# Sums of squares from the columns, the memory split ahead of the weights, and the weights' low part last

## The chip, the cores and the metric

The kernel runs on one core of a Trainium2 chip. The metric is the device time of one execution in microseconds. The engines are TensorE (PE; its weight loads are PEld), VectorE (DVE), ScalarE (ACT), GpSimd (POOL) and SyncE (SP), which here only issues loads.

## What is computed

One layer of a hybrid decoder for 256 tokens of width 2048, with 256 memory tokens, in float32. What matters here is the start:

```python
def rms_norm(x, w):
    xf = x.astype(jnp.float32)
    y = xf * lax.rsqrt(jnp.mean(xf * xf, axis=-1, keepdims=True) + NORM_EPS)
    return (y * w.astype(jnp.float32)).astype(x.dtype)
...
        h = rms_norm(x, norm_w[layer])
        proj = h @ w_in[layer]
...
        mem_n = rms_norm(mem, mem_norm_w[layer])
        o_mem = memory_cross_attention(mem_q..., mem_n, w_mem_kv[layer])
```

`memory_cross_attention` multiplies `mem_n` by `w_mem_kv` (2048 x 2048; the left half gives the keys, the right half the values). After that come a stick-breaking attention, a state-space branch, three gates, an output projection with a residual, and a last norm. The change touches none of those.

## The kernel before

**Products.** Every float32 matrix is split into a high part that TensorE takes as it is and a low part, the rest. A product is three: high by high, high by low, low by high. `split` (L142) does it: ScalarE copies the high part (L146), VectorE subtracts it from the source (L150, or L152 with a scale). For weights these tiles are `raw`, `wh` and `wl` (four buffers of `raw`, three of each of the others).

**Order.** The order of the work on each engine is that of the program (`manual_schedule`). The program is cut into chunks: one load of 512 KB of weights, its split, its products, and then a call of `pump` (L185), which runs the side work that has come due. `defer(fn, n)` (L172) puts a function n pumps ahead. A list `lanes` holds generators of which one step runs at every second pump.

**The start.** The memory and x lie transposed in 16 tiles of 128 features by 256 tokens, here called columns 0 to 15. ScalarE's queue loads `head` (the gains `memw` and memory column 0, `mem0`) and then memory columns 1, 2 to 3 and 4 to 5 (`mload`, L491 to L493). TensorE runs ten products of ones meanwhile (`keep_warm`, L108). `gemm_values` (L437) then makes the values in 16 steps k, each with 128 rows of the weights for all 1024 value columns: SyncE loads the weights (L446, for k=0 in two halves `g`), `split` splits them, and between or after that `along(k)` (L416) splits the memory's columns of step k and starts other loads. The products run over both halves g and both token blocks t, three for each (L456 to L458), twelve a step. The accumulators are two of TensorE's accumulator tiles.

**The norms.** The memory's and x's row scales are not applied to the factors but later. For them `row_squares` loads mem and x a second time, by rows (`load_rows`, L368, on ScalarE's queue), ScalarE squares and sums them (`squares`, L380), and `scale_steps` (L384) makes the mean, raises it to the power -1/2 on GpSimd (128x2, L389), multiplies it into a diagonal (`dg`, L393), and spreads it over the partitions with a product by ones (`rbc`, L396), copied to `rbc_m` or `rbc_x` (L398). `rs_mem`, one scale per row, is used when the values leave their accumulators (`to_split_rows`, L288, three and four pumps after the last step). `rbc_x` scales the columns of x (`scale_pair`, L474), which are then split into `hT` (`split_pair`).

**After that** two sets of eight chunks make the keys (`gemm`, L249, lines L269 to L271) and the next ones take `hT`. A chunk there holds two steps of k for 512 columns and has 12 products as well.

Of the kernel before, what the change touches and what calls it, by code (L numbers as in the profile page):

```python
# [41 lines left out]
def trunk_kernel(  # L42
# [55 lines left out]
    ones = const.tile([P, P], F32, name="ones")  # L98
    nc.gpsimd.memset(ones, 1.0)
    ident = const.tile([P, P], F32, name="ident")  # L100
# [22 lines left out]
                            pattern=[[1, P]], channel_multiplier=-1)  # L123

    rs_mem = const.tile([P, 2], F32, name="rs_mem")
    rs_x = const.tile([P, 2], F32, name="rs_x")
# [15 lines left out]
    def split(*parts):  # L142


        for hi, _, src, scale in parts:
            nc.scalar.activation(hi, src, AF.Copy, **({} if scale is None else {"scale": scale}))  # L146
        for hi, lo, src, scale in parts:
            h32 = hi.bitcast(F32)
            if scale is None:
                nc.vector.tensor_tensor(lo, src, h32, ALU.subtract)  # L150
            else:
                nc.vector.scalar_tensor_tensor(lo, src, scale, h32, ALU.mult, ALU.subtract)  # L152
# [212 lines left out]
    def split_cols(raw, dst, w, k0):  # L365
        split(*[(*dst.at(k), raw[k // 8][:, k % 8], w[:, k:k + 1]) for k in (k0, k0 + 1)])

    def load_rows(src, q):  # L368

        cs = slice(q * GW, (q + 1) * GW)  # L370
        if q % 2:
            r = [ta([P, GW], "rows") for _ in range(2)]
            for t in range(2):
                nc.scalar.dma_start(r[t], src[t * P:(t + 1) * P, cs])
            return r
        r = t4([P, 2, GW], "rows")
        nc.scalar.dma_start(r, src[:, cs].rearrange("(t p) n -> p t n", p=P))
        return [r[:, t] for t in range(2)]

    def squares(r, ss, q):  # L380
        for t in range(2):
            nc.scalar.activation(r[t], r[t], AF.Square, accum_out=ss[:, t, q:q + 1])

    def scale_steps(rs, rbc, ss):  # L384

        ms = small([P, 2], "ms")
        nc.vector.tensor_reduce(ms, ss, AX.X, ALU.add)
        nc.vector.tensor_scalar(ms, ms, 1.0 / D, EPS, ALU.mult, ALU.add)
        nc.gpsimd.tensor_tensor(rs, ms, mhalf, ALU.pow)  # L389
        yield  # L390
        dg = tq([P, 2, P], "dg")
        for t in range(2):
            nc.vector.tensor_scalar(dg[:, t], ident, rs[:, t:t + 1], None, ALU.mult)  # L393
        yield
        pb = bank([P, T], "rbc")
        nc.tensor.matmul(pb, ones, dg.rearrange("p t k -> p (t k)"), start=True, stop=True)  # L396
        yield
        nc.vector.tensor_copy(rbc, pb)  # L398
        yield


    memT = Cols(NKT, "memT")
    hT = Cols(NKT, "hT")
    mraw, mload = load_cols(mem_cols[:, NKT:], "mraw")
    xraw, xload = load_cols(x_cols, "xraw")
    ss_m = const.tile([P, 2, 4], F32, name="ss_m")
    ss_x = const.tile([P, 2, 4], F32, name="ss_x")

    vh = slot([P, 2, 1024], F32R, "vh")
    vl = slot([P, 2, 1024], F32R, "vl")  # L410

    def row_squares(src, ss, q):
        r = load_rows(src, q)
        defer(lambda: squares(r, ss, q), 3)

    def along(k):  # L416

        if k == 0:
            split((*memT.at(0), mem0, memw[:, 0:1]))
        else:  # L420
            split((*memT.at(k), mraw[k // 8][:, k % 8], memw[:, k:k + 1]))
            if k % 2 and 1 < k < 12:
                mload(k + 3, k + 5)
            if k % 2 and 3 <= k < 10:
                row_squares(mem, ss_m, k // 2 - 1)
            if k in (10, 12, 13, 14):
                row_squares(x, ss_x, (10, 12, 13, 14).index(k))
        if k == 6:
            nc.sync.dma_start(wcols, w_cols)
        if k == 12:  # L430
            defer(lambda: lanes[0].append(scale_steps(rs_mem, rbc_m, ss_m)), 1)
        if k == NKT - 2:
            defer(lambda: scale_x(scale_steps(rs_x, rbc_x, ss_x)), 3)
            for q in range(0, NKT, 4):
                defer(lambda q=q: xload(q, q + 4), 1 + q // 2)

    def gemm_values():  # L437

        acc = [psA.tile([P, 2, GW], F32, tag="acc", name=nm("acc"), bufs=2) for _ in range(2)]
        for k in range(NKT):  # L440
            raw, wh, wl = (stage.tile([P, 2, GW], dt, tag=n, name=nm(n), bufs=b) for n, dt, b in
                           (("raw", F32, RAWB), ("wh", F32R, 3), ("wl", F32R, 3)))
            src = w_mem_kv[k * P:(k + 1) * P, 1024:2048].rearrange("p (g n) -> p g n", n=GW)
            parts = [slice(0, 1), slice(1, 2)] if k == 0 else [slice(0, 2)]
            for g in parts:
                nc.sync.dma_start(raw[:, g], src[:, g])  # L446
            for n, g in enumerate(parts):
                split((wh[:, g], wl[:, g], raw[:, g], None))
                if n == 0:
                    along(k)  # L450
            lh, ll = memT.at(k)
            first, last = k == 0, k == NKT - 1
            for g in range(2):
                for t in range(2):
                    a, tt = acc[g][:, t], slice(t * P, (t + 1) * P)
                    nc.tensor.matmul(a, lh[:, tt], wh[:, g], start=first, stop=False)  # L456
                    nc.tensor.matmul(a, lh[:, tt], wl[:, g], start=False, stop=False)  # L457
                    nc.tensor.matmul(a, ll[:, tt], wh[:, g], start=False, stop=last)  # L458
            pump()
        for g in range(2):  # L460
            defer(lambda g=g: to_split_rows(vh, vl, g * GW, rs_mem)(
                [acc[g][:, t] for t in range(2)]), LATE + g)

    x_ready = []

    def scale_x(steps):

        for _ in steps:
            defer(lambda: scale_x(steps), 1)
            return  # L470
# [18 lines left out]
    head = tb([P, NKT + T], "head")  # L489
    memw, mem0 = head[:, 0:NKT], head[:, NKT:]  # L490
    nc.scalar.dma_start(head, mem_cols[:, 0:NKT + T])  # L491
    for k0, k1 in ((1, 2), (2, 4), (4, 6)):
        mload(k0, k1, nc.scalar)  # L493
    nc.scalar.preload_act_table_set("silu_and_others")

    gemm_values()
# [302 lines left out]
    pair = []  # L799
# [259 lines left out]
    g = 3  # L1059
# [60 lines left out]
```

## Time and profile before

| | us |
|---|---|
| median of 3 runs (1211.16 to 1211.69) | 1211.44 |
| the profiled execution | 1211.59 |
| its span | 1209.9 |
| TensorE busy in it | 1199.0 |
| first useful product (k=0) | 6.08 |
| first product of k=1 | 10.36 |
| first product of k=2 | 14.03 |

The span runs from the first to the last instruction. A row of the timeline gives the start, the duration, the engine, the line in the kernel, the operation, out<-in by the program's names, the size, and in brackets how long the engine stood idle before and what released it. A row of waits reads "who waited <- for what: total, times, longest". Rows of groups end in busy time, mean ns of one operation and idle time before. A DMA queue's row gives packets, MB and the share of the 16 DMA engines; q1 is SyncE's queue, q10 ScalarE's. A row by windows gives for a stretch its length, the busy time of PE, PEld, DVE, ACT and POOL, the granted TensorE clock, the DMA share and GB/s. All times are microseconds from the start of the span.

### The profile page before, as it was taken

The numbers are of one execution on the slowest core, as the hardware profiler recorded it, in microseconds if no ns is written. First come the engines' busy times: TensorE is split into PE (matmuls) and PEld (weight loads), VectorE is DVE, ScalarE is ACT, GpSimd is POOL, SyncE is SP. The second block draws the span as 40 slices with busy tenths as digits, with TensorE's granted clock in tenths as the row PEclk, the third lists the DMA queues.
The fourth block names the chain that finished last, engine by engine and source line by source line (L and its number), as shares of the span: only waits on it lengthen the run. The fifth ranks groups of instructions, "written<-read, shape, count | busy, mean of one in ns | idle before, by whom it ended". The sixth has DMA issues, their size and how long they took to land.

```text
span 1209.9 us, 15621 instructions
## 1 busy us (share of the span) xinstructions
PE 1199.0 (99%) x5820; PEld 1005.8 (83%) x5820; DVE 791.6 (65%) x1035; ACT 634.1 (52%) x844; POOL 52.5 (4%) x50
## 2 busy tenths in 40 slices
PE   9999999999999999999999999999999999999997
PEld 7888888888888888888888888888888888888886
DVE  5686664546564555888887858677777655556752
ACT  6754443354355444545655756484757534444541
POOL 0100000000000000010100000000000010110101
PEclk9999999999999999999999999999999999999999
DMA  9977787887666777665668676667756677778751
GB/s 320 363 229 228 215 244 235 251 232 214 197 192 194 218 224 226 185 189 169 180 179 261 210 226 214 212 204 220 229 177 202 204 221 222 228 219 293 252 203 70
DMA packets 169820, 264.66 MB, mean 219 GB/s; under 512 B 11984, under 2 KB 67472, under 8 KB 169616
## 3 DMA queue, kind: packets, MB, share of 16 engines
q1 hardware_dynamic: 134304, 227.41, 61.6%
q10 hardware_dynamic: 35440, 36.26, 9.2%
q8 instruction: 45, 0.74, 0.2%
q14 instruction: 31, 0.25, 0.1%
HBM read 249.45 MB, written 14.19 MB: 218 GB/s over the span
## 4 chain that ended last, share of the span: by engine, by line
PE 97%; issue 1%; DMA 1%; ACT 0%; DVE 0%; SPq 0%; POOLq 0%; POOL 0%; ACTq 0%
PE acc L269 25%; PE acc L271 25%; PE acc L270 25%; PE acc L229 10%; PE acc L233 5%; PE acc L457 1%; PE acc L458 1%; PE acc L456 1%; PE y L874 1%; DMA raw<-in_w_mem_kv_dram 1%; PE dtp L518 0%; PE acc L1074 0%; PE acc L1072 0%; PE acc L1073 0%; PE spo L708 0%
## 5 line engine op out<-in xcount | busy, mean ns | idle before, releaser
L150 DVE TENSOR_TENSOR wl<-raw,wh 128x1024 fp32r<-128x1024 f32 (+1 forms) x409 | 504.4, 1236 | 309.4 <-ACT wh L146 307.9
L146 ACT ACTIVATE wh<-raw 128x1024 fp32r<-128x1024 f32 (+1 forms) x409 | 431.4, 1056 | 426.8 <-PE acc L271 337.1
L269 PE MATMUL acc<-wh,hT 128*128 128x512 f32 x896 | 350.9, 392 | 0.0
L270 PE MATMUL acc<-wl,hT 128*128 128x512 f32 x896 | 348.9, 389 | 0.3 <-DVE wl L150 0.3
L271 PE MATMUL acc<-wh,hT 128*128 128x512 f32 x896 | 348.9, 389 | 0.0
L271 PEld LDWEIGHTS acc<-wh,hT 128*128 128x128 f32 x896 | 168.2, 188 | 35.4
L270 PEld LDWEIGHTS acc<-wl,hT 128*128 128x128 f32 x896 | 168.3, 188 | 34.4 <-DVE wl L150 0.7
L269 PEld LDWEIGHTS acc<-wh,hT 128*128 128x128 f32 x896 | 168.3, 188 | 33.9 <-issue 0.3
L229 PE MATMUL acc<-hT,wh 128*128 128x512 f32 x512 | 161.6, 397 | 0.0
L233 PEld LDWEIGHTS acc<-hT,wl 128*128 128x128 f32 x512 | 96.2, 188 | 22.7
L233 PE MATMUL acc<-hT,wl 128*128 128x256 f32 x512 | 100.7, 278 | 0.0
L229 PEld LDWEIGHTS acc<-hT,wh 128*128 128x128 f32 x512 | 78.1, 189 | 0.1
L269 PE MATMUL acc<-wh,oD 128*128 128x512 f32 x128 | 49.8, 389 | 0.0
L270 PE MATMUL acc<-wl,oD 128*128 128x512 f32 x128 | 49.8, 389 | 0.0
L271 PE MATMUL acc<-wh,oD 128*128 128x512 f32 x128 | 49.8, 389 | 0.0
L748 DVE SCALAR_TENSOR_TENSOR cT<-cu,wcols,cT 128x255 f32<-128x255 f32 (+2 forms) x96 | 46.4, 483 | 3.4
L963 POOL TENSOR_TENSOR merged<-merged,sig 128x512 f32<-128x512 f32 x16 | 25.8, 1637 | 512.3 <-DVE sig L962 512.3
L269 PE MATMUL acc<-wh,mT 128*128 128x512 f32 x96 | 37.4, 390 | 0.0
L271 PE MATMUL acc<-wh,mT 128*128 128x512 f32 x96 | 37.4, 389 | 0.0
L270 PE MATMUL acc<-wl,mT 128*128 128x512 f32 x96 | 37.4, 389 | 0.0
L689 POOL TENSOR_TENSOR lm<-lm,sp 128x384 f32<-128x384 f32 x8 | 11.5, 1433 | 391.6 <-DVE sp L688 389.5
L269 PEld LDWEIGHTS acc<-wh,oD 128*128 128x128 f32 x128 | 24.0, 188 | 5.0
(243 smaller groups left out, 1298.8 us busy)
## 6 DMA issues: line engine op xcount, KB each, us to landing
raw<-in_w_in_dram SPq DMA_DIRECT2D x288, 512.0 KB, 4.4
raw<-in_w_branch_ssd_dram SPq DMA_DIRECT2D x32, 512.0 KB, 4.9
raw<-in_w_mem_kv_dram SPq DMA_DIRECT2D x31, 512.0 KB, 6.0
raw<-in_w_out_dram SPq DMA_DIRECT2D x24, 512.0 KB, 5.6
scratch<-blocks ACTq DMA_DIRECT2D x23, 512.0 KB, 4.2
raw<-in_w_branch_mem_dram SPq DMA_DIRECT2D x16, 512.0 KB, 4.9
raw<-in_w_branch_sb_dram SPq DMA_DIRECT2D x16, 512.0 KB, 5.0
turned<-scratch ACTq DMA_DIRECT2D x60, 128.0 KB, 4.6
```

Of the source, the lines that this page charges most:

```text
L146: nc.scalar.activation(hi, src, AF.Copy, **({} if scale is None else {"scale": scale}))
L150: nc.vector.tensor_tensor(lo, src, h32, ALU.subtract)
L229: nc.tensor.matmul(halves[b], wh[:, kt - k0, b * P:(b + 1) * P], lhs.both(kt), start=first, stop=False, skip_group_check=True)
L233: nc.tensor.matmul(halves[b][:, 1], wl[:, kt - k0, b * P:(b + 1) * P], lhs.at(kt)[0], start=False, stop=last, skip_group_check=True)
L269: nc.tensor.matmul(a, lh[:, tt], wh[:, j], start=first, stop=False)
L270: nc.tensor.matmul(a, lh[:, tt], wl[:, j], start=False, stop=False)
L271: nc.tensor.matmul(a, ll[:, tt], wh[:, j], start=False, stop=last)
L456: nc.tensor.matmul(a, lh[:, tt], wh[:, g], start=first, stop=False)
L457: nc.tensor.matmul(a, lh[:, tt], wl[:, g], start=False, stop=False)
L458: nc.tensor.matmul(a, ll[:, tt], wh[:, g], start=False, stop=last)
L748: nc.vector.scalar_tensor_tensor(a[:, s:T], u[:, 0:T - s], convw[:, 3 - s, i:i + 1], a[:, s:T], ALU.mult, ALU.add)
L963: nc.gpsimd.tensor_tensor(merged[t][:, cs], merged[t][:, cs], sig[:, t], ALU.add)
```

## The change

1. The row loads and their squares go. ScalarE squares the columns that are loaded anyway, two steps of k at a time (`add_squares`); VectorE adds the squares up. One product by ones then gives every partition the sums of all rows. VectorE makes the mean from the accumulator, and GpSimd raises it to -1/2 for 256 columns, with three pumps before the next step. For the memory, VectorE then takes the row scales out of this by a product with the identity and a reduction (`rows_mem`).
2. In each step the memory is split ahead of the weights. For k=0 VectorE makes the high part itself. The weights of k=0 and k=1 are split in halves (those of k=1 arrive in one load).
3. The products with the weights' low part come last in each step; for k=0 the first half keeps them second.
4. ScalarE's queue loads only `head` and memory columns 1; the other memory columns come on SyncE's queue behind the weights of steps 1, 2, 3, 5, 7, 9 and 11. The columns of x are loaded at steps 6, 8, 10 and 12 instead of behind step 14, and the gain columns (`wcols`) at step 9 instead of 6.
5. The values leave their accumulators six and seven pumps after the last step instead of three and four. One more product of ones runs at the start (`WARM`).

```diff
-WARM = 10
+WARM = 11
...
-    def load_rows(src, q):
...
-    def squares(r, ss, q):
...
-    def scale_steps(rs, rbc, ss):
-
-        ms = small([P, 2], "ms")
-        nc.vector.tensor_reduce(ms, ss, AX.X, ALU.add)
-        nc.vector.tensor_scalar(ms, ms, 1.0 / D, EPS, ALU.mult, ALU.add)
-        nc.gpsimd.tensor_tensor(rs, ms, mhalf, ALU.pow)
-        yield
-        dg = tq([P, 2, P], "dg")
-        for t in range(2):
-            nc.vector.tensor_scalar(dg[:, t], ident, rs[:, t:t + 1], None, ALU.mult)
+    def add_squares(sq, pair, i):
+
+        r = sq if i == 0 else ta([P, 2, T], "sqs")
+        nc.scalar.activation(r, pair, AF.Square)
+        if i:
+            defer(lambda: nc.vector.tensor_tensor(sq, sq, r, ALU.add), 1)
+
+    def scale_steps(rbc, sq):
+
+        nc.vector.tensor_tensor(sq[:, 0], sq[:, 0], sq[:, 1], ALU.add)
         yield
         pb = bank([P, T], "rbc")
-        nc.tensor.matmul(pb, ones, dg.rearrange("p t k -> p (t k)"), start=True, stop=True)
-        yield
-        nc.vector.tensor_copy(rbc, pb)
-        yield
+        nc.tensor.matmul(pb, ones, sq[:, 0], start=True, stop=True)
+        yield
+        nc.vector.tensor_scalar(rbc, pb, 1.0 / D, EPS, ALU.mult, ALU.add)
+        nc.gpsimd.tensor_tensor(rbc, rbc, mhalf[:, 0:1].to_broadcast([P, T]), ALU.pow)
+        for _ in range(3):
+            yield
+
+    def soon(steps, then):
+
+        for _ in steps:
+            defer(lambda: soon(steps, then), 1)
+            return
+        then()
...
+    def rows_mem():
+
+        d = sq_m.rearrange("p a (t c) -> p (a t) c", c=P)[:, 0:2]
+        nc.vector.tensor_tensor(d, rbc_m.rearrange("p (t c) -> p t c", c=P),
+                                ident.unsqueeze(1).to_broadcast([P, 2, P]), ALU.mult)
+        nc.vector.tensor_reduce(rs_mem, d, AX.X, ALU.add)
...
     def along(k):
 
-        if k == 0:
-            split((*memT.at(0), mem0, memw[:, 0:1]))
-        else:
-            split((*memT.at(k), mraw[k // 8][:, k % 8], memw[:, k:k + 1]))
...
+        if 0 < k < 3 or k in (3, 5, 7, 9, 11):
+            k0 = 2 * k if k < 4 else k + 3
+            mload(k0, k0 + 2)
+        if k == 1:
+            nc.scalar.activation(sq_m[:, 0], mem0, AF.Square)
+            nc.scalar.activation(sq_m[:, 1], mraw[0][:, 1], AF.Square)
+        elif k in (3, 5, 7, 9, 11, 12, 14):
+            mem_pair(k // 2)
+        if k in (6, 8, 10, 12):
+            xload(2 * k - 12, 2 * k - 8)
+        if k == 9:
             nc.sync.dma_start(wcols, w_cols)
...
+        if k == 10:
+            for i in range(8):
+                defer(lambda i=i: x_pair(i), 1 + i)
+            defer(lambda: soon(scale_steps(rbc_x, sq_x), scale_x), 10)
+        if k == 14:
+            defer(lambda: soon(scale_steps(rbc_m, sq_m), rows_mem), 2)
...
+            hi, lo = memT.at(k)
+            part = mem0 if k == 0 else mraw[k // 8][:, k % 8]
+            if k == 0:
+                nc.vector.tensor_scalar(hi, part, memw[:, 0:1], None, ALU.mult)
+                split((wh[:, 0], wl[:, 0], raw[:, 0], None))
+                nc.vector.scalar_tensor_tensor(lo, part, memw[:, 0:1], hi.bitcast(F32),
+                                               ALU.mult, ALU.subtract)
+                split((wh[:, 1], wl[:, 1], raw[:, 1], None))
+            else:
+                split((hi, lo, part, memw[:, k:k + 1]))
+                for g in parts:
+                    split((wh[:, g], wl[:, g], raw[:, g], None))
+            along(k)
+            hh, hl, lh = (hi, wh), (hi, wl), (lo, wh)
+            order = ([(0, hh), (0, hl), (0, lh), (1, hh), (1, lh), (1, hl)] if k == 0 else
+                     [(g, pair) for pair in (hh, lh, hl) for g in range(2)])
...
-    for k0, k1 in ((1, 2), (2, 4), (4, 6)):
-        mload(k0, k1, nc.scalar)
+    mload(1, 2, nc.scalar)
```

More of the change, by code (lines that the diff above doesn't have):

```diff
@@ L125, in trunk_kernel @@
     rs_mem = const.tile([P, 2], F32, name="rs_mem")
-    rs_x = const.tile([P, 2], F32, name="rs_x")
     rbc_m = const.tile([P, T], F32, name="rbc_m")
@@ L366, in split_cols @@
         split(*[(*dst.at(k), raw[k // 8][:, k % 8], w[:, k:k + 1]) for k in (k0, k0 + 1)])
-    def load_rows(src, q):
-        cs = slice(q * GW, (q + 1) * GW)
-        if q % 2:
-            r = [ta([P, GW], "rows") for _ in range(2)]
-            for t in range(2):
[L374 to L378, printed above, removed]
-    def squares(r, ss, q):
-        for t in range(2):
-            nc.scalar.activation(r[t], r[t], AF.Square, accum_out=ss[:, t, q:q + 1])
-    def scale_steps(rs, rbc, ss):
-        ms = small([P, 2], "ms")
-        nc.vector.tensor_reduce(ms, ss, AX.X, ALU.add)
-        nc.vector.tensor_scalar(ms, ms, 1.0 / D, EPS, ALU.mult, ALU.add)
-        nc.gpsimd.tensor_tensor(rs, ms, mhalf, ALU.pow)
-        yield
-        dg = tq([P, 2, P], "dg")
-        for t in range(2):
-            nc.vector.tensor_scalar(dg[:, t], ident, rs[:, t:t + 1], None, ALU.mult)
+    def add_squares(sq, pair, i):
[5 more added lines that the diff above has]
+        nc.vector.tensor_tensor(sq[:, 0], sq[:, 0], sq[:, 1], ALU.add)
         yield
         pb = bank([P, T], "rbc")
-        nc.tensor.matmul(pb, ones, dg.rearrange("p t k -> p (t k)"), start=True, stop=True)
+        nc.tensor.matmul(pb, ones, sq[:, 0], start=True, stop=True)
         yield
-        nc.vector.tensor_copy(rbc, pb)
-        yield
+        nc.vector.tensor_scalar(rbc, pb, 1.0 / D, EPS, ALU.mult, ALU.add)
[7 more added lines that the diff above has]
+        then()
     memT = Cols(NKT, "memT")
@@ L405, in trunk_kernel @@
     xraw, xload = load_cols(x_cols, "xraw")
-    ss_m = const.tile([P, 2, 4], F32, name="ss_m")
-    ss_x = const.tile([P, 2, 4], F32, name="ss_x")
+    sq_m = tq([P, 2, T], "sq_m")
+    sq_x = tq([P, 2, T], "sq_x")
     vh = slot([P, 2, 1024], F32R, "vh")
     vl = slot([P, 2, 1024], F32R, "vl")
-    def row_squares(src, ss, q):
-        r = load_rows(src, q)
-        defer(lambda: squares(r, ss, q), 3)
-    def along(k):
-        if k == 0:
-            split((*memT.at(0), mem0, memw[:, 0:1]))
-        else:
-            split((*memT.at(k), mraw[k // 8][:, k % 8], memw[:, k:k + 1]))
[L422 to L428, printed above, removed]
-            nc.sync.dma_start(wcols, w_cols)
[L430 to L435, printed above, removed]
@@ new lines, in rows_mem, with mem_pair, x_pair @@
+    def rows_mem():
[3 more added lines that the diff above has]
+        nc.vector.tensor_reduce(rs_mem, d, AX.X, ALU.add)
+    def mem_pair(i):
+        add_squares(sq_m, mraw[i // 4][:, 2 * i % 8:2 * i % 8 + 2], i)
+    def x_pair(i):
+        add_squares(sq_x, xraw[i // 4][:, 2 * i % 8:2 * i % 8 + 2], i)
+    def along(k):
+        if 0 < k < 3 or k in (3, 5, 7, 9, 11):
[9 more added lines that the diff above has]
+        if k == 9:
+            nc.sync.dma_start(wcols, w_cols)
+        if k == 10:
[4 more added lines that the diff above has]
+            defer(lambda: soon(scale_steps(rbc_m, sq_m), rows_mem), 2)
@@ L443, in gemm_values @@
             src = w_mem_kv[k * P:(k + 1) * P, 1024:2048].rearrange("p (g n) -> p g n", n=GW)
-            parts = [slice(0, 1), slice(1, 2)] if k == 0 else [slice(0, 2)]
-            for g in parts:
+            parts = [slice(0, 1), slice(1, 2)] if k < 2 else [slice(0, 2)]
+            for g in parts if k == 0 else [slice(0, 2)]:
                 nc.sync.dma_start(raw[:, g], src[:, g])
[L447 to L453, printed above, removed]
+            hi, lo = memT.at(k)
[14 more added lines that the diff above has]
+                     [(g, pair) for pair in (hh, lh, hl) for g in range(2)])
+            for i, (g, (a, w)) in enumerate(order):
                 for t in range(2):
[L455 to L458, printed above, removed]
+                    nc.tensor.matmul(acc[g][:, t], a[:, t * P:(t + 1) * P], w[:, g],
+                                     start=(k == 0 and i in (0, 3)),
+                                     stop=(k == NKT - 1 and i > 3))
             pump()
@@ L461, in gemm_values, with scale_x @@
             defer(lambda g=g: to_split_rows(vh, vl, g * GW, rs_mem)(
-                [acc[g][:, t] for t in range(2)]), LATE + g)
+                [acc[g][:, t] for t in range(2)]), 6 + g)
     x_ready = []
[L466 to L470, printed above, removed]
+    def scale_x():
         for k in range(0, NKT, 2):
```

## The prediction

> **What bounds the kernel now.** I read the page first (busy shares, the chain that ended last), then TensorE's waits, then the timelines of the opening microseconds, then the DMA queues there.
>
> ```profile
> PE 1199.0 (99%) x5820; PEld 1005.8 (83%) x5820; DVE 791.6 (65%) x1035; ACT 634.1 (52%) x844; POOL 52.5 (4%) x50
> PE 97%; issue 1%; DMA 1%; ACT 0%; DVE 0%; SPq 0%; POOLq 0%; POOL 0%; ACTq 0%
> PE acc L456 <- ACT memT L146: 0.9, 2, 0.5
> PE acc L457 <- DVE wl L150: 0.5, 2, 0.4
> PE acc L270 <- DVE wl L150: 0.3, 1, 0.3
> ```
>
> TensorE is busy 99% of the span and is 97% of the chain. Apart from its start, it waits in three groups, of which only the first two (the memory-value products, L456 and L457) lie where the change works. So a gain can only come from the opening, and a loss can come from any new wait of TensorE behind it.
>
> ```profile
> 1.06 4.64 PE L110 MATMUL warm<-ones 128*128 128x128 f32 x20 [1.06 <-POOL ones L99]
> 6.08 0.51 PE L456 MATMUL acc<-wh,memT 128*128 128x512 f32 x1 [0.39 <-ACT memT L146]
> 10.36 0.49 PE L456 MATMUL acc<-wh,memT 128*128 128x512 f32 x1 [0.54 <-ACT memT L146]
> 14.03 0.39 PE L456 MATMUL acc<-wh,memT 128*128 128x512 f32 x1
> 52.11 0.39 PE L269 MATMUL acc<-wh,memT 128*128 128x512 f32 x1
> ```
>
> 6.08 is the first useful product, 10.36 the first of step k=1, 14.03 the first of k=2, 52.11 the first after the value products. From 14.03 on, 14 steps of 12 products take 38.08 us, 0.227 each: no gap. A step at that pace lasts 2.72 us, so the first two, which took 14.03 - 6.08 = 7.95, hold 2.5 us of waiting. That is nearly all that can be won.
>
> ```profile
> 5.00 0.63 ACT L146 ACTIVATE wh<-raw 128x512 fp32r<-128x512 f32 x1 [1.03 <-DMA raw<-in_w_mem_kv_dram]
> 5.54 0.49 ACT L146 ACTIVATE memT<-head 128x256 fp32r<-128x256 f32 x1
> 6.99 0.63 ACT L146 ACTIVATE wh<-raw 128x512 fp32r<-128x512 f32 x1 [0.96 <-DMA raw<-in_w_mem_kv_dram]
> 8.86 1.06 ACT L146 ACTIVATE wh<-raw 128x1024 fp32r<-128x1024 f32 x1 [1.23 <-DMA raw<-in_w_mem_kv_dram]
> 9.82 0.49 ACT L146 ACTIVATE memT<-mraw,head 128x256 fp32r<-128x256 f32 x1
> 5.67 0.69 DVE L150 TENSOR_TENSOR wl<-raw,wh 128x512 fp32r<-128x512 f32 x1 [5.67 <-ACT wh L146]
> 6.28 0.48 DVE L152 SCALAR_TENSOR_TENSOR memT<-head,memT 128x256 fp32r<-128x256 f32 x1
> ```
>
> The weights of k=0 land in halves just before 5.00 and 6.99, those of k=1 just before 8.86. Behind each landing stand the whole weight split and then the memory split on ScalarE: k=1 lands at 8.83 but starts at 10.36.
>
> **The change part by part.** *Opening order.* The memory's high part of k=0 goes to VectorE, ready at about 5.17 (below) + 0.42 = 5.6, so the first product waits for wh at 5.63 alone. But an eleventh warm-up product is added. The twenty half-products start (4.64 - 0.42)/19 = 0.222 apart, so the last of 22 starts at 5.72 and the first useful one can start at 5.94 (now 6.08). The low part of the weights ends at 5.67 + 0.69 = 6.36 and that of the memory at 6.28 + 0.48 = 6.76, as now. The six products of the first half go 5.94, 6.17, 6.42 (waits wl), 6.76, 6.99, 7.22, and the second half can start at 7.45 if its weights have landed by 7.45 - 0.63 - 0.08 = 6.74. Then k=1 could start at 7.45 + 6 x 0.227 = 8.82. Its memory is split beforehand and its weights in halves, so it needs landing + 0.03 + 0.63 + 0.05: by 8.1 at the latest. The products with wl come last, 1.8 us later, and hide the subtractions (0.69 each).
>
> *Loads.* Two 256 KB loads of memory columns leave ScalarE's queue and go behind the weights of k=1 and k=2 on SyncE's.
>
> ```profile
> q10 hardware_dynamic: 346, 0.39, 19.3%
> q10 hardware_dynamic: 480, 0.63, 22.8%
> q1 hardware_dynamic: 301, 1.02, 68.8%
> q10 hardware_dynamic: 317, 0.47, 33.9%
> SPq L446 <- DMA head<-in_mem_cols_dram: 2.5, 1, 2.5
> 0.00:5.00 5.00, 3.94 (x18) 3.94 (x19) 0.00 (x0) 1.28 (x1) 1.95 (x14) 1.00 0.53 119
> ```
>
> These are ScalarE's queue (q10) from 0 to 6.96 and from 0 to 8.83, then SyncE's (q1) and ScalarE's from 5 to 8.83. Together they move (1.02 + 0.47)/3.83 = 0.39 MB/us. Only 0.27 MB of q10 (136 and 128 KB) stay ahead in the new order. So 0.12 MB are gone before the second half of k=0, which lands 0.3 earlier, at 6.65; and 0.36 MB before k=1, which lands 0.9 earlier, at 7.9. Both are inside the limits 6.74 and 8.1, by little. For k=2, 256 KB of memory are now ahead on q1, and the 512 KB taken off q10 more than pay for them; it must land by 10.4 and the same rate gives 10.1. The ninth load of the program waited for the first (the fifth row: SyncE stood 2.5 us until the head had landed, at 5.17); in the new order the ninth is k=3's weights, as now.
>
> Sum: k=2 starts at 8.82 + 2.72 = 11.54 instead of 14.03, a gain of 2.5; a product after a stall costs up to 0.11 more, so 2.3 to 2.5, and I take 2.4. Everything behind it is the same work at the same pace and moves with it.
>
> *Squares.* Row loads (4 MB), 16 squares and 16 accumulator reads go; 17 squares, 14 sums and 2 joins come.
>
> ```profile
> L382 ACT ACTIVATE rows<-rows 128x512 f32<-128x512 f32 x16 | 10.0, 625 | 7.3 <-DMA rows<-in_x_dram 4.0 <-DMA rows<-in_mem_dram 3.3
> L476 DVE TENSOR_TENSOR xraw<-xraw,rbc_x 128x512 f32<-128x512 f32 x8 | 5.5, 687 | 0.0
> L150 DVE TENSOR_TENSOR wl<-raw,wh 128x1024 fp32r<-128x1024 f32 x44 | 53.7, 1222 | 36.8 <-ACT wh L146 36.6
> L152 DVE SCALAR_TENSOR_TENSOR memT<-mraw,head,memT 128x256 fp32r<-128x256 f32 x15 | 7.2, 478 | 0.0
> ```
>
> ScalarE does 15 x 0.63 + 2 x 0.49 = 10.4 us for 10.0 and the reads: nothing on the path. VectorE gets 14 x 0.69 = 9.6 us. In steps 12 to 16 its load is 1.22 + 0.48 + 0.69 and a memory sum every other step, 2.4 to 3.1 us against 2.72: its lead covers that; without it, some 0.3 us. The x loads, moved from behind the weights to steps 6 to 12, make 1.75 MB per two steps (5.44 us), 0.32 MB/us, under the 0.39: nothing. The scaling of x begins four chunks later and its last split stands right before the chunk that uses it; VectorE then has about 35 us of work in 14 chunks (38 us): nothing, or up to 1 us if it has lost its lead. The diagonal products and copies that go are 1 us of VectorE, hidden as well.
>
> *The power.* This is the open cost. It was 128x2 on GpSimd, twice; now it is 128x256, twice, and behind the first stand the two VectorE operations that make the rows' scales (about 0.42 each, as a copy of that size).
>
> ```profile
> L389 POOL TENSOR_TENSOR rs_x<-ms,mhalf 128x2 f32<-128x2 f32 x1 | 0.7, 702 | 8.5 <-DVE ms L388 8.5
> L1014 POOL TENSOR_TENSOR frs<-msy,mhalf 128x1 f32<-128x1 f32 x2 | 1.4, 676 | 18.4 <-DVE msy L1009 18.4
> L995 POOL TENSOR_TENSOR yo<-yo,fw 128x512 f32<-128x512 f32 x6 | 7.7, 1298 | 56.4 <-ACT junk L994 56.4
> 398.21 1.02 POOL L689 TENSOR_TENSOR lm<-lm,sp 128x384 f32<-128x384 f32 x1 [219.60 <-DVE sp L688]
> 42.99 1.61 POOL L389 TENSOR_TENSOR rs_mem<-ms,mhalf 128x2 f32<-128x2 f32 x1 [40.23 <-DVE ms L388]
> 43.95 0.48 DVE L152 SCALAR_TENSOR_TENSOR memT<-mraw,head,memT 128x256 fp32r<-128x256 f32 x1
> 875.16 3.54 POOL L963 TENSOR_TENSOR merged<-merged,sig 128x512 f32<-128x512 f32 x2 [33.30 <-DVE sig L962]
> 875.89 1.65 DVE L150 TENSOR_TENSOR wl<-raw,wh 128x1024 fp32r<-128x1024 f32 x1 [0.28 <-ACT wh L146]
> 877.46 1.79 DVE L855 TENSOR_TENSOR dec<-dec,cbs 128x512 f32<-128x512 f32 x1
> ```
>
> Lower end: plain operations cost (1.298 - 1.02)/128 = 2.2 ns a column, so 0.70 + 254 x 2.2 ns = 1.3 us. Upper end: the second column of a power cost 0.702 - 0.676 = 26 ns, and 254 of these make 0.70 + 6.6 = 7.3 us; if the one-column rows hold a wait, the step and the price are larger, and no row excludes that. One and two columns cost nearly the same, which is the sign of a start-up, so I take the low end, weakly. Three chunks (8.2 us) are left between power and use, so even 7.3 would not make the user wait. The Trainium skill's GPSIMD Engine Reference (Performance versus the Vector engine) gives about 12 cycles an element for data-dependent code at 1.2 GHz, 10 ns a column, an estimate of 3.2 us, by which the first rival below would give 1210.7; it prices no power, and no run here shows that figure.
>
> **The rivals.** *The power holds the port.* At 875 VectorE's subtraction took 1.65 instead of 1.22 and the next operation 1.79 instead of 0.69: each ended as if it had started only when GpSimd's operation was over. The same page (Specifications) says that GpSimd shares its SBUF interfaces with VectorE, in contention with operations of two SBUF inputs; for plain operations this trace agrees. Against it for the power: at 43.95 VectorE's two-input operation ran its usual 0.48 while the power of 42.99 was open until 44.60, so a power of two columns left the port.
>
> ```profile
> 61.36 0.42 DVE L398 COPY rbc_x<-rbc 128x256 f32<-128x256 f32 x1 [1.26 <-PE rbc L396]
> 72.31 1.06 ACT L146 ACTIVATE wh<-raw 128x1024 fp32r<-128x1024 f32 x1 [1.66 <-PE acc L271]
> 73.40 1.22 DVE L150 TENSOR_TENSOR wl<-raw,wh 128x1024 fp32r<-128x1024 f32 x1 [0.89 <-ACT wh L146]
> ```
>
> VectorE can't build up cover: with three buffers ScalarE's split waits for TensorE (72.31), and wl ends at 74.6, 2.9 us before its chunk. And VectorE stands at the broadcast sums until TensorE's product is through (61.36), 3.4 us after the start of chunk 0. It then does the step and wl of chunk 2 (to 4.8), the power takes the port, and the sum and wl of chunk 3 (0.6 + 1.2) must end by 8.8: a power of up to 2.2 us is free. At the second power the same count gives 2.7. Above that each microsecond is TensorE's, twice: 2p - 4.9. It cancels the gain at p = 3.65; at 7.3 it costs 9.7, and the time is 1218.9.
>
> *The weights land no earlier.* If SyncE's queue runs no faster alone, the landings stay at 6.96 and 8.83, k=1 starts at 9.54 and k=2 at 12.37: gain 1.7, 1209.9. For it: until 5 us the two queues together move only 119 GB/s (the last row of the loads), though both have loads issued, so something other than their sharing holds them. This is also the case in which the change, as a relief of the queue, doesn't do what it says.
>
> **How the numbers follow.** The profiled execution took 1211.59 (span 1209.9; the median is 1211.44, 0.15 less). 1211.59 - 2.4 = 1209.2. What a measurement of this kernel can tell is about 0.2%, 2.4 us, so the forecast itself lies on that bound. Forecast, alone 1208.8 to 1209.6: 0.42, of which I put 0.20 beyond 0.2% and 0.22 within it. Late weights: 0.12, within it. The port rival: 0.40; of this 0.08 with p between 2.2 and 4.8 and a time within 0.2%, 0.32 slower. Other losses (x scaling late, a power of over 8.2 us without the port): 0.06, slower 0.04, within 0.02. Together: faster 0.20, same 0.44, slower 0.36. The range reaches from 1208.6 to 1219.0, which takes in the port rival up to the upper price; what is dearer still is left out, at less than 0.2.
>
> **What would show it.** Right: first product near 5.94, k=1 near 8.8, k=2 near 11.5, TensorE then without waits; ScalarE's waits for raw at k=1 end near 7.9. Wrong: GpSimd rows of several microseconds near 54 and 66 us, VectorE subtractions of the same length beside them, and TensorE waits on wl of L150 in chunks 3 and 7 of the key products. If the second half of k=0 still lands at 6.96, the queue step was wrong.

## The result, and the profile after

The changed kernel takes 1277.14 us (median of 5, 1276.64 to 1277.64), the kernel before 1211.44 (median of 5, 1211.16 to 1212.45). The ratio is 1.0539, 95% interval 1.0527 to 1.0551: 5.4% slower, far outside the forecast range. The profiled execution took 1276.64 with a span of 1274.9, which is 65.0 more than before.

The page of the changed kernel (busy time by engine; then the chain that ended last):

```profile
PE 1202.6 (94%) x5822; PEld 1009.0 (79%) x5822; DVE 800.9 (63%) x1047; ACT 632.2 (50%) x829; POOL 133.3 (10%) x50
PE 91%; POOL 7%; issue 1%; DVE 1%; ACT 0%; POOLq 0%; ACTq 0%
```

GpSimd goes from 52.5 us busy to 133.3 with the same number of instructions, and 7% of the chain is now its own. TensorE's waits:

```profile
PE acc L269 <- DVE wl L149: 63.3, 3, 33.1
```

The small waits of the opening are gone (only the start before the first warm-up product is left). In their place stand 63.3 us in three waits for a weights' low part; the shortest of them, 0.3, stood in the kernel before too. The timeline around the two long ones, GpSimd, VectorE and TensorE together:

```profile
53.77 42.05 POOL L382 TENSOR_TENSOR rbc_m<-rbc_m,mhalf 128x256 f32<-128x256 f32 x1 [51.03 <-DVE rbc_m L381]
54.74 1.10 DVE L372 TENSOR_TENSOR sq_x<-sq_x,sqs 128x512 f32<-128x512 f32 x1
57.23 1.21 DVE L149 TENSOR_TENSOR wl<-raw,wh 128x1024 fp32r<-128x1024 f32 x1
95.86 0.43 DVE L407 TENSOR_TENSOR sq_m<-rbc_m,ident 128x256 f32<-128x256 f32 x1 [37.41 <-POOL rbc_m L382]
96.66 1.22 DVE L149 TENSOR_TENSOR wl<-raw,wh 128x1024 fp32r<-128x1024 f32 x1
97.92 0.80 PE L269 MATMUL acc<-wl,memT 128*128 128x512 f32 x1 [33.12 <-DVE wl L149]
99.89 42.04 POOL L382 TENSOR_TENSOR rbc_x<-rbc_x,mhalf 128x256 f32<-128x256 f32 x1 [4.07 <-DVE rbc_x L381]
141.97 0.73 DVE L483 TENSOR_TENSOR xraw<-xraw,rbc_x 128x512 f32<-128x512 f32 x1 [34.04 <-POOL rbc_x L382]
143.89 0.80 PE L269 MATMUL acc<-wl,memT 128*128 128x512 f32 x1 [29.93 <-DVE wl L149]
```

Read it from the bottom of each group upwards. TensorE stands 33.12 us for `wl`. VectorE makes that `wl` in 1.22 us as ever, but it stands in VectorE's order behind `rows_mem` (L407), which needs the power's result and has itself waited 37.41 us. The power lasts 42.05. The second power does the same to the scaling of x (L483). VectorE works at its usual 1.21 beside the power (57.23). Only the addition right behind the power's start (54.74) took 1.10, where one of that size took 0.68 in a kernel without the power (the one with Ln and Exp, below). So VectorE is not slowed by more than 0.4 us; it is queued behind one instruction that waits.

Behind each wait the products start 0.427 apart in place of 0.227:

```profile
98.52 0.63 PE L270 MATMUL acc<-wh,memT 128*128 128x512 f32 x1
98.94 0.63 PE L268 MATMUL acc<-wh,memT 128*128 128x512 f32 x1
...
102.65 0.40 PE L268 MATMUL acc<-wh,memT 128*128 128x512 f32 x1
```

By windows of 1 us (the number behind the busy times is the granted clock):

```profile
64.00:65.00 1.00, 0.81 (x4) 0.36 (x2) 0.00 (x0) 0.00 (x0) 1.00 (x1) 1.00 0.00 0
68.00:69.00 1.00, 0.00 (x0) 0.00 (x0) 0.00 (x0) 0.00 (x0) 1.00 (x1) 0.67 0.00 0
101.00:102.00 1.00, 1.00 (x4) 0.74 (x3) 1.00 (x2) 0.09 (x1) 1.00 (x1) 0.50 0.02 6
103.00:104.00 1.00, 1.00 (x6) 0.82 (x5) 0.45 (x2) 0.91 (x1) 1.00 (x1) 1.00 0.87 295
```

The clock falls to half some 3.5 us after TensorE's last product (at 64.81) and comes back 4.5 us after the restart. From 97.92 to 102.65 eleven products take 4.73 us instead of 2.5, 2.2 more; behind the second wait it is 1.5 more. The Trainium skill, "TensorE: Matmul & The Clock Gate" (Part 1), says that TensorE falls to half its clock after an idle window of about 3.4 us; the first wait agrees with that.

The opening, TensorE's and ScalarE's rows:

```profile
5.77 1.20 PE L466 MATMUL acc<-wh,memT 128*128 128x512 f32 x2
6.77 0.69 PE L466 MATMUL acc<-wl,memT 128*128 128x512 f32 x2
9.11 1.98 PE L466 MATMUL acc<-wh,memT 128*128 128x512 f32 x8
11.83 0.84 PE L466 MATMUL acc<-wh,memT 128*128 128x512 f32 x3
6.67 0.63 ACT L145 ACTIVATE wh<-raw 128x512 fp32r<-128x512 f32 x1 [1.08 <-DMA raw<-in_w_mem_kv_dram]
7.98 1.16 ACT L145 ACTIVATE wh<-raw 128x512 fp32r<-128x512 f32 x2 [0.28 <-DMA raw<-in_w_mem_kv_dram]
```

k=2 starts at 11.83 instead of 14.03: 2.2 us are won, where 2.4 were forecast. The account: 63.0 us of new waits, 3.7 of half pace, less 2.2, is 64.5 of the 65.0.

### The profile page after: what moved, and what is told of

Its sections match the earlier page's. It is cut to its first block, busy times and chain, and to the rows that moved or that the text cites. A ratio compares the mean times of both kernels' runs of the same rounds, so it can differ in the third digit from the quotient of the medians.

```text
span 1274.9 us, 15615 instructions
## 1 busy us (share of the span) xinstructions
PE 1202.6 (94%) x5822; PEld 1009.0 (79%) x5822; DVE 800.9 (63%) x1047; ACT 632.2 (50%) x829; POOL 133.3 (10%) x50
## 4 chain that ended last, share of the span: by engine, by line
PE 91%; POOL 7%; issue 1%; DVE 1%; ACT 0%; POOLq 0%; ACTq 0%
PE acc L268 23%; PE acc L269 23%; PE acc L270 23%; PE acc L228 9%; PE acc L232 5%; PE acc L466 3%; POOL rbc_m L382 3%; POOL rbc_x L382 3%; PE y L880 1%; PE warm L110 0%; DVE wl L149 0%; PE dtp L524 0%; PE acc L1079 0%; PE acc L1078 0%; PE acc L1080 0%
## 5 line engine op out<-in xcount | busy, mean ns | idle before, releaser
L269 PE MATMUL acc<-wl,memT 128*128 128x512 f32 x64 | 26.8, 419 | 63.1 <-DVE wl L149 63.1
L269 PEld LDWEIGHTS acc<-wl,memT 128*128 128x128 f32 x64 | 12.9, 202 | 66.6 <-DVE wl L149 63.9
L382 POOL TENSOR_TENSOR rbc_m<-rbc_m,mhalf 128x256 f32<-128x256 f32 x1 | 42.0, 42050 | 51.0 <-DVE rbc_m L381 51.0
L382 POOL TENSOR_TENSOR rbc_x<-rbc_x,mhalf 128x256 f32<-128x256 f32 x1 | 42.0, 42042 | 4.1 <-DVE rbc_x L381 4.1
```

What stands on the lines that cost most here:

```text
L269: nc.tensor.matmul(a, lh[:, tt], wl[:, j], start=False, stop=False)
L382: nc.gpsimd.tensor_tensor(rbc, rbc, mhalf[:, 0:1].to_broadcast([P, T]), ALU.pow)
```

## The experiments

Two theories stood against each other; the expectations name them by letters. U: the power itself lasts 42 us, at so much a column, and the loss is that its users wait. P: the power is long, and it costs because it holds VectorE's port while it runs. A third question was whether the opening's gain came from where the prediction had put it (Q: the queue that the loads stand in). Each ratio below is to the kernel before on the same chip.

**The power on two columns again.** Everything of the change stays, but the row sums are taken into one column per token block, raised to the power there, and spread over the partitions afterwards, as before the change:

```diff
-        nc.tensor.matmul(pb, ones, sq[:, 0], start=True, stop=True)
+        for t in range(2):
+            nc.tensor.matmul(pb[:, T + t:T + t + 1], sq[:, 0, t * P:(t + 1) * P], ones[:, 0:1],
+                             start=True, stop=True)
...
-        nc.gpsimd.tensor_tensor(rbc, rbc, mhalf[:, 0:1].to_broadcast([P, T]), ALU.pow)
+        nc.gpsimd.tensor_tensor(rs, ms, mhalf, ALU.pow)
...
+            nc.vector.tensor_scalar(dg[:, t], ident, rs[:, t:t + 1], None, ALU.mult)
...
+        nc.tensor.matmul(pb[:, :T], ones, dg.rearrange("p t k -> p (t k)"), start=True, stop=True)
```

> The changed kernel, but each row's sum comes out of two one-column products and the power is taken of 128x2 as before the change, then spread by the diagonal and the product by ones. Theory U (TensorE lost 63 us because the next user of a 42 us power waits for it): 1209.3, the opening's 2.2 us below 1211.44, no wait of TensorE after the opening. Theory P (a large part was lost to GpSimd holding VectorE's port): the same here, since the power is 0.7 us again. Theory O (the other edits cost as well, so the power is not all): above 1211.

It took 1210.3 us, ratio 0.9988 (0.9979 to 0.9997). The 65 us are gone with the size of the power, and TensorE has no wait over 0.3 us behind its start. It misses the 1209.3 by 1.0; the row sums are not free, as TensorE's rows show (0.36 for the row sums, and the next product follows late too):

```profile
52.46 0.50 PE L381 MATMUL rbc<-ones,sq_m 128*128 128x1 f32 x4
52.82 0.49 PE L269 MATMUL acc<-wh,memT 128*128 128x512 f32 x1
53.15 0.40 PE L270 MATMUL acc<-wl,memT 128*128 128x512 f32 x1
```

From 52.46 to 53.15 there is one product at 0.227 and 0.46 us more, twice in the kernel: 0.9.

**Powers that nobody waits for.** The last kernel, with an unused power of 256 columns beside VectorE's full work, and further on unused powers of other sizes and one plain product:

```diff
+        defer(lambda: nc.gpsimd.tensor_tensor(dump[:, 0:256], rbc_x[:, 0:256], mhalf[:, 0:1].to_broadcast([P, 256]), ALU.pow), 1)
...
+        for n in (1, 2, 4, 16, 64):
+            nc.gpsimd.tensor_tensor(dump[:, 0:n], rbc_x[:, 0:n],
+                                    mhalf[:, 0:1].to_broadcast([P, n]), ALU.pow)
+        nc.gpsimd.tensor_tensor(dump, rbc_x, rbc_m, ALU.mult)
```

> r1_small_power with extra powers whose result nobody uses: one of 128x256 while VectorE is busiest with the keys, and later 1, 2, 4, 16 and 64 columns in a row. Theory U: the time of r1_small_power within 1 us; the powers take 0.37 + 0.163 us a column, so 0.53, 0.70, 1.0, 3.0, 10.8 and 42; VectorE's two-input subtractions beside the long one keep their 1.22 us. Theory P: VectorE's two-input operations beside it wait until it ends, and the kernel is some 35 us longer.

It took 1210.39, ratio 0.9987 (0.9978 to 0.9996): the same as without them. The groups by shape (busy us, mean ns of one), GpSimd:

```profile
L482 POOL TENSOR_TENSOR dump<-rbc_x,mhalf 128x256 f32<-128x256 f32 x1 | 42.0, 42037 | 7.4 <-DVE rbc_x L395 7.4
L737 POOL TENSOR_TENSOR dump<-rbc_x,mhalf 128x64 f32<-128x64 f32 x1 | 10.5, 10518 | 0.1
L737 POOL TENSOR_TENSOR dump<-rbc_x,mhalf 128x16 f32<-128x16 f32 x1 | 3.8, 3792 | 0.1
L737 POOL TENSOR_TENSOR dump<-rbc_x,mhalf 128x1 f32<-128x1 f32 x1 | 1.6, 1628 | 0.0
L739 POOL TENSOR_TENSOR dump<-rbc_x,rbc_m 128x256 f32<-128x256 f32 x1 | 1.1, 1072 | 0.1
L737 POOL TENSOR_TENSOR dump<-rbc_x,mhalf 128x4 f32<-128x4 f32 x1 | 1.0, 1007 | 0.1
L737 POOL TENSOR_TENSOR dump<-rbc_x,mhalf 128x2 f32<-128x2 f32 x1 | 0.7, 711 | 0.1
```

The same 256 columns cost 1.07 us as a plain product and 42.04 as a power. From 64 to 256 columns it is (42.04 - 10.52)/192 = 0.164 us a column, from 2 to 4 it is 0.148. The powers of 1 and of 16 columns lie above this line; both were issued while VectorE ran a subtraction (until 178.79 and 182.20), the ones of 2, 4 and 64 were not. The one of 256 was issued 1.06 us ahead of such an end (75.53); without this 1.06 the slope to 256 is 0.159. And VectorE, beside the unused power (74.47 to 116.5):

```profile
74.31 1.22 DVE L151 TENSOR_TENSOR wl<-raw,wh 128x1024 fp32r<-128x1024 f32 x1
75.44 1.10 DVE L488 TENSOR_TENSOR xraw<-xraw,rbc_x 128x512 f32<-128x512 f32 x1
76.47 1.21 DVE L151 TENSOR_TENSOR wl<-raw,wh 128x1024 fp32r<-128x1024 f32 x1
```

One operation near the power's start took 1.10 instead of 0.69; all later ones had their usual times. P falls as the cause of the loss: VectorE lost 0.4 us beside the power, and a power of 42 us that nobody waits for costs nothing that can be measured in the whole time.

**Between the two sizes.** If only the users' wait counts, there must be a size that fits into the slack. These two kernels are the changed kernel with the power over the first 40 and the first 96 of the 256 columns; the other scales stay without the root, so they leave out that part of the norms.

```diff
-        nc.gpsimd.tensor_tensor(rbc, rbc, mhalf[:, 0:1].to_broadcast([P, T]), ALU.pow)
+        nc.gpsimd.tensor_tensor(rbc[:, 0:40], rbc[:, 0:40],
+                                mhalf[:, 0:1].to_broadcast([P, 40]), ALU.pow)
```

> The changed kernel with the power taken of only 40 of the 256 columns (the other rows keep their mean square as scale, so this leaves out part of the norms). Theory U: a power of 6.9 us, inside the cover that the changed kernel's trace shows (42.05 - 33.1 = 8.9 us at the first, 42.04 - 29.9 = 12.1 at the second), so 1209.3. Theory P: twice the power less 4.9, 8.9 us more, 1218.

> The changed kernel with the power taken of 96 columns (the other rows keep their mean square as scale). Theory U: 16.0 us each, 7.1 and 3.9 beyond the cover, 1209.3 + 11 = 1220, and up to 2 more where TensorE comes back at half clock. Theory P: 2 x 16 - 4.9 = 27 more, 1236.

40 columns: 1209.24, ratio 0.9979 (0.997 to 0.9988). GpSimd's first power (TensorE's only wait behind the start is 0.3 us):

```profile
53.78 7.67 POOL L382 TENSOR_TENSOR rbc_m<-rbc_m,mhalf 128x40 f32<-128x40 f32 x1 [51.04 <-DVE rbc_m L381]
```

96 columns: 1225.75, ratio 1.0117 (1.0103 to 1.013). Its first power and the two waits that follow from the two powers:

```profile
53.74 16.55 POOL L382 TENSOR_TENSOR rbc_m<-rbc_m,mhalf 128x96 f32<-128x96 f32 x1 [50.99 <-DVE rbc_m L381]
72.39 0.80 PE L269 MATMUL acc<-wl,memT 128*128 128x512 f32 x1 [7.62 <-DVE wl L149]
92.86 0.79 PE L269 MATMUL acc<-wl,memT 128*128 128x512 f32 x1 [3.81 <-DVE wl L149]
```

In one place and kernel, 40, 96 and 256 columns give 7.67, 16.55 and 42.05: 0.159 us a column in both steps, on 1.3. Of the first power 16.55 - 7.62 = 8.9 us are free, and from the 256 columns 42.05 - 33.12 = 8.9 again; of the second 12.7 and 12.1. So the user begins to wait at about (8.9 - 1.3)/0.159 = 48 columns. The 96 columns took more than U's figure (1220, and up to 2 more for the half clock): the time is 16.5 above that of 40 columns, of which the waits (12.2 in all, 0.3 at 40 columns) are 11.9. The rest fits the clock. The trace is that of the slowest of four executions, 1227.5, which is 17.9 above the trace with 40 columns. It shows a granted clock of 0.59 from 70 to 80 us and of 0.66 from 90 to 100: TensorE works at half clock for 5.9 us behind each wait and loses 5.9 us in all, and 11.9 + 5.9 is 17.8. The other three have a mean granted clock of 0.994, this one 0.991.

**The same values without a power.** ScalarE makes exp(-ln(m)/2) from the accumulator, and one Newton step (a square on ScalarE, two operations on VectorE) brings it to full precision; ScalarE's table of functions is exchanged once more (1.28 us).

```diff
-        nc.vector.tensor_scalar(rbc, pb, 1.0 / D, EPS, ALU.mult, ALU.add)
-        nc.gpsimd.tensor_tensor(rbc, rbc, mhalf[:, 0:1].to_broadcast([P, T]), ALU.pow)
+        nc.scalar.activation(rbc, pb, AF.Ln, scale=1.0 / D, bias=eps[:, 0:1])
+        nc.scalar.activation(rbc, rbc, AF.Exp, scale=-0.5)
...
+        nc.scalar.activation(neg, pb, AF.Identity, scale=-1.0 / D, bias=eps[:, 1:2])
+        nc.scalar.activation(half, rbc, AF.Square, scale=0.5 ** 0.5)
+        nc.vector.tensor_tensor(half, half, neg, ALU.mult)
...
+        nc.vector.scalar_tensor_tensor(rbc, half, 1.5, rbc, ALU.add, ALU.mult)
```

> The changed kernel with the 256-column power replaced by a logarithm, an exponential and one Newton step on ScalarE and VectorE, four pumps before the use; no extra product. Theory U: no wait of TensorE behind the opening and, without the row sums that take 0.47 us of TensorE twice in r1_small_power, 0.9 us below that: 2.4 under the time before, 1209.0 to 1209.4. Rival S: r1_small_power stood above r3_power_40 only by scatter of the landings, and this comes out at 1210.3 too. If ScalarE's four operations hold up the weight splits, TensorE waits in chunks 2 to 4 of the keys, up to 1.2 us.

It took 1209.57 (1209.14 to 1210.11), ratio 0.9981 (0.9973 to 0.999): 0.2% below the kernel before, with an interval that ends just under 1. From the first row below (the logarithm, 53.18) to the second (VectorE's last, which ends at 58.54) are 5.4 us, inside the 8.9 that are free.

```profile
53.18 0.47 ACT L382 ACTIVATE rbc_m<-rbc,eps 128x256 f32<-128x256 f32 x1 [3.06 <-PE rbc L379]
58.12 0.42 DVE L390 SCALAR_TENSOR_TENSOR rbc_m<-sq_m,rbc_m 128x256 f32<-128x256 f32 x1
```

The other experiments take the opening apart. Three of them undo one part each in the kernel with the small power (1210.3; weights' second half split from 6.53, k=1 weights from 7.89, products of k=1 at 8.94 and k=2 at 11.66). These are the times of one execution, and they scatter: over the seven traces with the changed kernel's opening, the split of the second half starts at 6.41 to 7.07, that of the weights of k=1 at 7.74 to 8.42, and k=2 at 11.64 to 12.02. The latest each time is the kernel with unused powers, whose first extra operation comes at 74.47.

**The loads on ScalarE's queue again.**

```diff
-        if 0 < k < 3 or k in (3, 5, 7, 9, 11):
+        if k in (3, 5, 7, 9, 11):
...
-    mload(1, 2, nc.scalar)
+    for k0, k1 in ((1, 2), (2, 4), (4, 6)):
+        mload(k0, k1, nc.scalar)
```

> r1_small_power with memory columns 2 to 5 back on ScalarE's queue at the start, as before the change. Theory Q (both queues share one rate, so these 512 KB push the weights back): the second half of k=0 lands 0.3 later, k=1's weights 0.9 later (at 8.8), the first product of k=2 0.7 to 0.9 later than the 11.7 of r1_small_power, and the time 0.8 above it. Rival L (the landings do not depend on that queue): as r1_small_power.

It took 1210.93, ratio 0.9994 (0.9985 to 1.0003). ScalarE's and TensorE's rows:

```profile
7.11 0.63 ACT L146 ACTIVATE wh<-raw 128x512 fp32r<-128x512 f32 x1 [1.44 <-DMA raw<-in_w_mem_kv_dram]
9.04 1.15 ACT L146 ACTIVATE wh<-raw 128x512 fp32r<-128x512 f32 x2 [0.89 <-DMA raw<-in_w_mem_kv_dram]
12.63 0.39 PE L469 MATMUL acc<-wh,memT 128*128 128x512 f32 x1
```

The second half of k=0 lands 0.6 later and the weights of k=1 1.15 later, and k=2 starts 0.97 later. Against the latest of the seven traces it is 0.04, 0.62 and 0.61. So the loads on the other queue did hold the weights of k=1 back, as the queue step had it; for the second half of k=0 these traces can't tell. In the whole time it is 0.6 us, inside the two intervals.

**The low part second again**, as before the change: `order = [(g, pair) for g in range(2) for pair in (hh, hl, lh)]`.

> r1_small_power with the products of the weights' low part second in every step, as before the change. If the new order hides the subtraction: at k=1 TensorE waits for it 0.7 us after the high part, k=2 starts 0.5 to 0.9 later than 11.7, the time 0.5 to 0.9 above r1_small_power. Rival: with the memory split ahead the order no longer matters, no difference.

It took 1210.67, ratio 0.9992 (0.9983 to 1.0), and k=2 starts at about 11.7, as with the low part last. This part of the change is worth nothing that can be measured here.

**The memory's split behind the weights' again**, from k=1 on:

```diff
-                split((hi, lo, part, memw[:, k:k + 1]))
                 for g in parts:
                     split((wh[:, g], wl[:, g], raw[:, g], None))
+                split((hi, lo, part, memw[:, k:k + 1]))
```

> r1_small_power with the memory split behind the weights from k=1 on. If the split ahead matters: k=1 waits for both weight halves and the memory's high part, about 1.0 us more than in r1_small_power, k=2 starts that much later, the time 0.8 to 1.0 above. Rival: the landing of k=1 ends the wait anyway, and it is within 0.2.

It took 1211.11, ratio 0.9995 (0.9986 to 1.0004). TensorE waits for `memT` again at k=1, and k=2 starts 0.55 later, though the weights landed no later (split from 7.73; in the kernel with Ln and Exp they are split from 7.74, and k=2 starts at 11.69):

```profile
9.34 2.12 PE L469 MATMUL acc<-wh,memT 128*128 128x512 f32 x8 [0.22 <-ACT memT L146]
12.21 0.84 PE L469 MATMUL acc<-wh,memT 128*128 128x512 f32 x3
```

**The opening alone.** The kernel before with the edits of its opening (numbers 2, 3 and the memory's loads of number 4, and 11 warm-up products); row loads, row squares and powers of two columns stay.

> The kernel before with the edits of the opening alone: the memory's split ahead of the weights', the products with the low part last, the memory's loads moved behind the weights', 11 warm-up products. The row loads, the row squares and the 128x2 powers stay. If the row loads and row squares cost the path nothing (as the prediction had it), the opening gains about the 2.2 us that the changed kernel gained and nothing is lost behind it: about 1209.3, with the step k=2 starting at 11.7 to 12.1 on the TensorE. Rival: the row loads, still issued beside the weights, hold the memory's or the weights' landings up, which the changed kernel was spared; then k=2 starts later than 12.3 or waits on a landing appear behind it, and the time is above 1210.3.

It took 1209.8, ratio 0.9988 (0.9979 to 0.9997), and k=2 starts at 11.89:

```profile
11.89 1.30 PE L463 MATMUL acc<-wh,memT 128*128 128x512 f32 x5
```

That is 0.5 above the first expectation, with the weights of k=1 split 0.2 later than in the changed kernel (8.18 beside 7.98), and k=2 inside the expected 11.7 to 12.1. So the opening's gain needs nothing of the new squares, and 4 MB of row loads cost no time that these runs can tell (1209.8 beside 1209.57 with Ln and Exp).

**Ten warm-up products** in the kernel with Ln and Exp (`WARM = 10`).

> The kernel with the Ln and Exp in place of the power, and 10 warm-up products in place of 11. If the first product waits for its operands and not for the warm-up products, nothing changes: within 0.3 us of the 1209.6 of the run with 11, first product at the same time or up to 0.2 us earlier. Rival: the clock is not up when the real products begin; then the first of them stand 0.43 us apart in place of 0.23 and the time is 1 us or more longer.

It took 1209.2 (1209.04 to 1209.6), ratio 0.9981 (0.9972 to 0.999). The first useful product starts at 5.77 as with eleven, k=2 at 11.92 instead of 11.69; the times differ by 0.4, and the ratios do not. The eleventh product neither helps nor harms. The sign that the rival named is there in part: the second and the third useful product start at 6.36 and 6.79, 0.43 apart, and the full pace begins near 7 us; but the time is not longer for it.

**The waits filled.** The changed kernel, with 140 and 128 unused products of ones by ones on TensorE where it waits for the powers.

```diff
     def rows_mem():
 
+        for _ in range(140):
+            nc.tensor.matmul(fill[0][:, 0:P], ones, ones, start=True, stop=True)
```

> The changed kernel with 140 and 128 unused products of ones by ones placed on the TensorE in the two waits for the power. The waits for the power stay as long as they are. If the half pace of the products behind each wait (0.43 us apart for some 4 us) comes from the TensorE having stood idle, the products behind the waits stand 0.23 us apart at once, and the time is about 3.6 us shorter than that of the changed kernel: about 1273.5. If the half pace has another cause (the weights' buffers, VectorE behind), it stays and the time is 1277.

It took 1275.86, ratio 1.0531 (1.0515 to 1.0547): 1.3 us less than the changed kernel by the medians, with intervals that overlap, and not the 3.6 expected. TensorE's rows and two windows behind the first wait:

```profile
97.77 0.50 PE L269 MATMUL acc<-wl,memT 128*128 128x512 f32 x1 [1.85 <-DVE wl L149]
143.74 0.50 PE L269 MATMUL acc<-wl,memT 128*128 128x512 f32 x1 [1.83 <-DVE wl L149]
147.46 0.50 PE L269 MATMUL acc<-wl,memT 128*128 128x512 f32 x1 [0.71 <-DVE wl L149]
```
```profile
98.00:99.00 1.00, 1.00 (x4) 0.81 (x4) 1.00 (x2) 1.00 (x2) 0.00 (x0) 0.72 0.16 29
99.00:100.00 1.00, 1.00 (x4) 0.72 (x3) 1.00 (x3) 1.00 (x3) 0.27 (x1) 0.50 0.81 258
```

Three things came between. TensorE was through with the fill 1.85 us too early, and the clock fell all the same for some 3.4 us. Behind the second wait the clock held, but VectorE, which had stood 34 us, was late with the next `wl` (0.71). And what is saved behind the first wait is lost again: the second wait ends with GpSimd's second power, and so only 0.15 us earlier (143.74 beside 143.89). The half pace is in the account of the 65 us, but it is not a cost that can be taken away by itself.

## Why the prediction was wrong

- **The step that failed is the price of the power.** "One and two columns cost nearly the same, which is the sign of a start-up, so I take the low end, weakly": 1.3 us was taken, 7.3 was the upper end, 42.05 was measured. The 26 ns of the second column was the difference of two rows of which one held a wait. The prediction said that such a wait would make the step larger and that no row excluded it, but did not look for it. The trace of before had it:

```profile
1192.89 0.42 DVE L1010 TENSOR_TENSOR yo<-yo,fw 128x256 f32<-128x256 f32 x1
1193.05 0.67 POOL L1014 TENSOR_TENSOR frs<-msy,mhalf 128x1 f32<-128x1 f32 x1 [9.09 <-DVE msy L1009]
42.81 1.23 DVE L150 TENSOR_TENSOR wl<-raw,wh 128x1024 fp32r<-128x1024 f32 x1
```

  The power of one column ends at 1193.72, 0.41 after VectorE's operation with two inputs (1193.31). That of two columns at 42.99, quoted in the prediction, ends at 44.60, 0.56 after VectorE's (44.04). Both seem to have waited for VectorE and then run; the second column is 0.56 - 0.41 = 0.15 us, not 0.026, and 254 of them on the 0.70 of two columns make 39 us. The run with unused powers fits: its one column took 1.63, more than its two (0.71), and ended 0.42 after VectorE's subtraction. That the wait is for the port was not tested by itself.
- **The condition was right, the size was not.** "Three chunks (8.2 us) are left between power and use, so even 7.3 would not make the user wait." 8.9 us were free, and a power of 7.67 made no one wait. With that size of power the whole time is 1209.24, beside the 1209.2 of the sum; that they meet to 0.04 is luck, since the interval of that run (0.997 to 0.9988) leaves 1.5 to 3.6 us for the gain. So the power is the only term that failed by more than some tenths; what became of it is the case named last, "a power of over 8.2 us without the port", at 0.04 for slower.
- **The main rival was wrong in its size.** The power doesn't hold the port for as long as it lasts: VectorE's addition right behind its start took 0.74, 0.83 and 1.10 us with 40, 96 and 256 columns, where 0.68 is usual. These 0.06, 0.15 and 0.42 us are 1.6 ns a column, near the 2.2 ns that the prediction found for a plain operation; the rest of the 42 us beside VectorE cost nothing. The rival's price (2p - 4.9, 79 us at p = 42) would not have given the 65 either.
- **The Trainium skill's figure.** The estimate of 3.2 us from "GPSIMD Engine Reference" (Performance versus the Vector engine) went by about 10 ns a column; the measurement is 159 ns, and it decides.
- **The opening was right.** The second half was there for a split at 6.67 (forecast 6.65), the weights of k=1 for 7.98 (7.9), k=1 started at 9.11 (8.82), k=2 at 11.83 (11.54): 2.2 won instead of 2.4. That the landings meet to 0.1 is partly luck: over the seven traces with this opening they scatter by 0.7, and in the latest the second half is split only from 7.07, no earlier than before the change (6.99). The 0.3 are lost in k=0: its twelve products took 3.34 us (5.77 to 9.11), where the sum had 2.88 with its stall for `wl`, and no wait is recorded there. Its first products start at 5.77, 6.34, 6.77 and 7.06, which is 0.57, 0.43 and 0.29 apart, and the next ones 0.23. TensorE was still at half its pace: the trace's record of the granted clock begins only at 6.89 us (the windows print 1.00 ahead of it). In the kernel with the small power the record begins at 4.67, and the warm-up half-products, 0.21 us apart until then, are 0.11 apart from there on. The sum took the full pace from the first useful product on. The queue step (for the weights of k=1) and the split ahead are shown in the start of k=2 by the two runs that undo them, and the whole time shows neither; the low part last was costed as a cover for the subtractions, and the run without it shows that no cover was needed.
- **Squares and loads cost nothing that shows**, as costed: 40 columns with all of them take what the sum says, within that run's interval.

## What to carry to other kernels

Price an operation at the size it will have by the slope between sizes, and before subtracting two rows look at what the engine that shares its memory was doing in each of them. Compare landing times with several traces of the same opening and not with one. When an operation's price is bounded only weakly, count the work that stands in order behind its first user: here one late row scale on VectorE held TensorE, since every later `wl` stood behind it. A reciprocal root over a whole tile went well as a logarithm and an exponential on ScalarE with a Newton step; on GpSimd it belongs on as few columns as the data allows.

## What the runs showed of the hardware

- A power on GpSimd takes 0.159 to 0.164 us for each column of 128 partitions; over 256 columns that is 39 times the plain product of the same size (42.04 against 1.07).
- It leaves VectorE's operations with two inputs at their pace but for the one right behind its start (0.06, 0.15 and 0.42 us longer with 40, 96 and 256 columns), where plain GpSimd operations had made them wait until they were over (1.65 and 1.79 at 875 us, in the prediction).
- TensorE's clock fell to half 3.5 us after the last product in the first wait, 2.2 us after it in the second, and once even when TensorE stood only 1.85 us (the filled kernel); another gap of 1.83 us left it whole. The Trainium skill, "TensorE: Matmul & The Clock Gate" (Part 1), speaks of an idle window of about 3.4 us; a shorter gap was enough here.
- The traces fit a clock that is set by fixed stretches of 3.41 us. Every stretch of half clock behind a wait lasts a whole multiple of that: 34.13 and 30.72 in the changed kernel, 10.24 and 6.83 with 96 columns, 3.41 in the filled one. Cut at these edges, the traces show the clock fall behind stretches in which TensorE was busy for 0, 5, 16, 37 and 46% of the time. The gap of 1.85 us lay inside one of them (95.02 to 98.44, 46%); that of 1.83 was split between two (139.40 to 146.22, 73% each), and the clock stayed. It came back behind stretches of 86% and more, and not behind two of 72% with 96 columns.
- TensorE starts at half pace as well. In the five traces whose clock record begins before 5.6 us the warm-up half-products go from 0.21 us apart to 0.11 just there. With the same opening the record begins anywhere from 4.61 to 6.89, so the kernel doesn't set it, and the start of k=2 holds some luck of 0.2 us.
